# A fifth row buffer for the whole kernel in place of a fourth pair of split trunk weights, tile 2's keys found beside its scores, and a closer plan for dense-stage rows

## The chip, the cores and the metric

One core of one Trainium2 chip. The metric is device time in microseconds, taken over several runs; a profile of one execution gives where it goes. TensorE (PE) multiplies matrices, VectorE (DVE), ScalarE (ACT) and GpSimd (POOL) work on tiles in on-chip memory, SyncE (SP) issues most transfers, and 16 DMA engines carry them. Each engine takes its own instructions in order and waits for others through semaphores.

## What is computed

One inference step of a one-layer hybrid model on 1024 prompt positions and 128 sample positions (9 tiles of 128 tokens; tile 0 is the sample). A trunk of large projections, gating and retention comes first, then a product-key retrieval over 16384 single-neuron experts. Of the latter:

```python
q = (t @ w_query).reshape(T, P_HEADS, P_DKEY)
s1 = jnp.einsum('thd,nd->thn', q[..., :P_HALF], k1)
s2 = jnp.einsum('thd,nd->thn', q[..., P_HALF:], k2)
v1, i1 = lax.top_k(s1, P_TOPK)
v2, i2 = lax.top_k(s2, P_TOPK)
cand = (v1[..., :, None] + v2[..., None, :]).reshape(T, P_HEADS, P_TOPK * P_TOPK)
vals, flat = lax.top_k(cand, P_TOPK)
...
a = jax.nn.gelu(jnp.einsum('td,thkd->thk', t, eu[experts]))
return jnp.einsum('thk,thkd->td', w * a, ev[experts])
```

Each token picks 8 x 16 = 128 experts, and each expert has a row of 1024 numbers in `eu` and one in `ev`.

## The kernel before

**Trunk.** The tiles go through in three groups: tiles 0 and 1, tiles 2 to 5, tiles 6 to 8. A group streams 128 weight units of 512 KB each. `take` (from L126) loads units ahead, splits each into a high and a low part (`whi` copied by ScalarE, `wlo` subtracted by VectorE, both in `split`, L200 and L204) and hands out the pair; three products on TensorE then stand for one of full precision. A unit of 512 columns is 24 products. Pairs are split up to unit n+2 when unit n is handed out, and `NPART` (L107) is the number of pairs that there is room for, 4. In the first group the row buffers `gat` also serve as places for raw weights (two units in each), so `n_raw` grows with their number `GB`.

**Two ways of retrieval.** For tiles 0, 1, 2, 6 and 7 the 128 experts of each token are gathered: step j (L786, issued by GpSimd) brings for each of 128 tokens one row of 2048 numbers, 1 MB in all, into a buffer `gat`; VectorE forms the dot product with the token (`dot`, L739), ScalarE the weight (`weigh`, L744 and L745), VectorE adds the weighted second half to `acc` (`add`, L749), and the buffer is free. That is 5 x 128 = 640 rows. Tiles 3, 4, 5 and 8 go through a dense stage at the end instead: for each of 128 blocks of 128 experts, 24 products (L1008) give the scores, these are multiplied by the retrieval weights, split, and 24 further products (L980) add to the outputs. A block's loads are 1 MB and an eighth of a 2 MB tile of weights.

**What sets the order.** The rows and the search for their experts are side work. Two lanes, `gather_all` and `prepare`, each carry a clock of planned microseconds; `advance` adds the trunk's or the dense stage's planned cost, and `run_side` lets a lane go on until its clock has caught up. A row counts `PACE` = 5.0 planned us; a dense block counts twice 5.12. That fixes the order in which the program is written. The scheduler of the framework then places instructions on the engines by priority and as buffers come free; dense work has a priority 200 instructions ahead, so rows fill what it leaves. A row's buffer is the resource that it has to wait for.

**Row buffers.** `GB` = 4 buffers `gat`, and `AHEAD` = 2: the dot product of a row follows two steps after its gather. From dense block 2 to dense block 124 in program order, `spare` gives a fifth buffer `gats` in the dense stage's own memory, taken by every fifth row of a tile, and `AHEAD` is 3.

**Keys.** `top_keys` finds the best 16 of 128 scores for both halves of a head with ten operations of VectorE and a cast. For the tiles in `EARLY` (0, 1 and 8) this is done in `scores` right where the query stage produces the scores; for the others the scores are stored (`ssp`), loaded back by `topk_units` and searched there, in the lane `prepare`. Its results `v12` and `i12` have two buffers.

Of the kernel before, what the change touches and what calls it, by code (L numbers as in the profile page):

```python
# [8 lines left out]
F32 = mybir.dt.float32  # L9
# [8 lines left out]
P = 128  # L18
D = 1024
# [3 lines left out]
PH, NKEYS, TOPK = 8, 128, 16  # L23
# [19 lines left out]

GATHER, DENSE = [0, 1, 2, 6, 7], [3, 4, 5, 8]

EARLY = [0, 1, 8]
TD = len(DENSE) * P
EC = 4
LT = 16
# [5 lines left out]
def step_kernel(ctx: ExitStack, tc: tile.TileContext, x, state, wall, wst, bs, rows, vec, cst, smp, cosd, sind, euv,  # L55
# [5 lines left out]
    peer = ctx.enter_context(tc.tile_pool(name="peer", bufs=1))  # L61
# [42 lines left out]
            order += [U_IN + 2 * (32 + cb), U_IN + 2 * (32 + cb) + 1, U_PA + 2 * cb, U_PA + 2 * cb + 1]  # L104
        order += [U_OUT + i for i in range(8)] + [U_Q + i for i in range(16)]
    per = len(order) // len(GROUPS)
    NRAW, NPART, NBK = 3, 4, 2  # L107
    GB = 4
    MIX = 3
    wst_ = {"take": 0, "load": 0, "split": 0}  # L110
    raws, parts = {}, {}
    n_raw = lambda n: 2 * GB + MIX if n < per - 2 else NRAW
    pair = None

    def load(n):
        nonlocal pair
        if n < per - 2 and n % 3 < 2:

            if n % 3 == 0:
                pair = peer.tile([P, 2, 4, 256], F32, name="gat", bufs=GB)  # L120
            t = pair[:, n % 3]
# [37 lines left out]
    def mm_us(n):  # L159
        return n / 2400.0  # L160
# [36 lines left out]
    def split(parts, src, scale=None):  # L197

        if scale is None:
            nc.scalar.copy(parts[0], src)  # L200
        else:
            nc.scalar.activation(parts[0], src, AF.Copy, scale=scale)
        if scale is None:
            nc.vector.tensor_tensor(parts[1], src, parts[0].bitcast(F32), op=OP.subtract)  # L204
        else:
            nc.vector.scalar_tensor_tensor(parts[1], src, scale, parts[0].bitcast(F32), op0=OP.mult, op1=OP.subtract)
# [377 lines left out]
    def query(gi, pl, tl, nt, T, tT, rs, unit):  # L584
        def scores(h, qh):
            for i, t in enumerate(tl):
# [5 lines left out]
                st = st.rearrange("p a b -> p (a b)")  # L592
                if t in EARLY:
                    top_keys(t, h, st)
# [20 lines left out]
            pass  # L615


    AHEAD = [2]
    PACE = [5.0]
    BOOST = [100]  # L620
    AB = 2
# [17 lines left out]
    def top_keys(t, h, src):  # L639

        if t not in early:
            early[t] = (peer.tile([P, 2, PH, TOPK], F32, name="v12", bufs=2),
                        peer.tile([P, 2, PH, TOPK], BF16, name="i12", bufs=2))
        v12, i12 = early[t]
        tmp = peer.tile([P, P], F32, name="ktmp")
        iu = peer.tile([P, 2, TOPK], U32, name="iu")
        for c in range(2):
            top16(src[:, c * P:(c + 1) * P], tmp, v12[:, c, h], iu[:, c])
        nc.vector.tensor_copy(i12[:, :, h], iu)
        keyed[t] = h + 1  # L650
# [84 lines left out]
    queue = []  # L735

    def dot(t, j, b):
        d = T_[t]
        nc.vector.tensor_tensor_reduce(out=b[:, :D], in0=b[:, :D], in1=d["x"], op0=OP.mult, op1=OP.add,  # L739
                                       scale=1.0, scalar=0.0, accum_out=d["s"][:, j:j + 1])  # L740

    def weigh(t, j, b):
        d = T_[t]
        nc.scalar.activation(d["s"][:, j:j + 1], d["s"][:, j:j + 1], AF.Gelu_apprx_tanh)  # L744
        nc.scalar.activation(d["s"][:, j:j + 1], d["s"][:, j:j + 1], AF.Copy, scale=d["w"][:, j:j + 1])  # L745

    def add(t, j, b):
        d = T_[t]
        nc.vector.scalar_tensor_tensor(d["acc"], b[:, D:], d["s"][:, j:j + 1], d["acc"], op0=OP.mult, op1=OP.add)  # L749
        if j == HK - 1:  # L750
            out_norm(d["acc"], peer.tile([P, 2 * D], F32, name="gat", bufs=GB), t)
            del T_[t]
# [3 lines left out]
    def gathered():  # L756

        last = list(dotted)
        dotted.clear()
        for cur in last:  # L760
            weigh(*cur)
        while len(queue) > AHEAD[0]:
            cur = queue.pop()
            if cur:
                dot(*cur)
                dotted.append(cur)
        for cur in last:
            add(*cur)

    spare = []  # L770

    def row_buffer(j):

        if spare and j % (GB + 1) == GB:
            return spare[0].tile([P, 2 * D], F32, name="gats", bufs=1)
        return peer.tile([P, 2 * D], F32, name="gat", bufs=GB)

    def gather(t):
        d = T_[t]
        d["x"] = peer.tile([P, D], F32, name="tx")  # L780
        nc.sync.dma_start(d["x"], tsp[t])
        d["acc"] = peer.tile([P, D], F32, name="acc", bufs=2)
        nc.sync.dma_start(d["acc"], xsp[t])
        for j in range(HK):
            b = row_buffer(j)
            nc.gpsimd.indirect_dma_start(out=b, out_offset=None, in_=euv,  # L786
                                         in_offset=bass.IndirectOffsetOnAxis(ap=d["idx"][:, j:j + 1], axis=0))
            queue.insert(0, (t, j, b))
            gathered()
            yield PACE[0]  # L790
# [55 lines left out]
    def out_norm(acc, tmp, t):  # L846

        nc.sync.dma_start(tmp[:, D:], row_bcast(rows, 2))
        final_norm(acc, tmp[:, :D], tmp[:, D:], t)
# [61 lines left out]
    def advance(c):  # L911
        nonlocal tm
        tm += c
        flush()
        run_side(tm)
# [31 lines left out]
    dp = dense_sb.enter_context(tc.tile_pool(name="dp", bufs=1))  # L947
# [9 lines left out]
    def fetch(name, e):  # L957
        if e < NKEYS:
            raw[name, e] = wp.tile([P, D], F32, name="wraw", bufs=RWB)
            nc.sync.dma_start(raw[name, e], eud[e].rearrange("p k e -> p (k e)") if name == "eu" else evd[e])  # L960

    def split_u(e):
        if e < NKEYS:
            eu[e] = [wp.tile([P, D], F32R, name=n, bufs=EUB) for n in ("whi", "wlo")]
            split(eu[e], raw.pop(("eu", e)))

    def split_v(e):
        r = raw.pop(("ev", e))
        ev[e] = []
        for j in range(2):  # L970
            h = [dp.tile([P, 512], F32R, name=f"ev{j}{m}", bufs=(2, NBK + 1)[j]) for m in range(2)]
            split(h, r[:, 512 * j:512 * j + 512])
            ev[e].append(h)
# [8 lines left out]
    def block(o, es):  # L982
        ps = dps.tile([P, 512], F32, name="blk")
        for e in es:
            value(ps, o, e, e == es[0], e == es[-1])
        if es[0] == 0:
            nc.vector.tensor_copy(oacc[o], ps)
        else:
            nc.vector.tensor_tensor(oacc[o], oacc[o], ps, op=OP.add)

    us = 24 * mm_us(TD)
    todo = []
    hp = ExitStack()
    hp.enter_context(tc.high_priority(DP))
# [4 lines left out]
    for e in range(NKEYS + 1):  # L999
        if e < NKEYS:  # L1000
            if e % BE == 0:
                pt = dp.tile([P, TD // LT, BE, LT], F32, name="pt", bufs=2)
                nc.sync.dma_start(pt.rearrange("p c e t -> p c (e t)"), pdr[e // BE])
            ps = dps.tile([P, TD], F32, name="S")
            for k in range(KD):
                w, a = [p[:, k * P:(k + 1) * P] for p in eu[e]], [p[:, k] for p in tT]
                for i, (x, y) in enumerate(((w[0], a[0]), (w[1], a[0]), (w[0], a[1]))):
                    mm(ps, x, y, start=k == 0 and i == 0, stop=k == KD - 1 and i == 2)  # L1008
            del eu[e]
            fetch("ev", e + 1)  # L1010
            fetch("eu", e + 2)
            a = dp.tile([P, TD], F32, name="a", bufs=2)
            nc.scalar.activation(a, ps, AF.Gelu_apprx_tanh)  # L1013
            r16 = lambda z: z.rearrange("p (c t) -> p c t", t=LT)
            nc.vector.tensor_tensor(r16(a), r16(a), pt[:, :, e % BE], op=OP.mult)
            G[e] = [dp.tile([P, TD], F32R, name=f"g{m}", bufs=NBK + 1) for m in range(2)]
            split(G[e], a)
            split_v(e)
            split_u(e + 2)
            if e == 2:  # L1020
                spare.append(dp)
                AHEAD[0] = 3
            if e == NKEYS - 4:
                spare.clear()
                AHEAD[0] = 2
            hp.close()
            advance(us)
            hp.enter_context(tc.high_priority(DP))
        if todo:
            block(*todo.pop())  # L1030
        if e:
            for o in held:
                value(res[o], o, e - 1, e == 1, e == NKEYS)
            if e % NBK == 0 or e == NKEYS:
                es = list(range((e - 1) // NBK * NBK, e))
                if len(blocked) > 0:
                    block(blocked[0], es)
                if len(blocked) > 1:
                    todo.append((blocked[1], es))
            hp.close()  # L1040
            advance(us)
            hp.enter_context(tc.high_priority(DP))
# [98 lines left out]
```

## Time and profile before

| | us |
|---|---|
| median of 3 runs | 4063.04 (4037.91 to 4064.33) |
| the profiled execution, its own time | 4061.48 |
| its span, first to last instruction | 4059.4 |
| TensorE busy | 3655.6 (90% of the span) |
| VectorE busy | 3459.1 (85%) |
| ScalarE busy | 1846.8 (45%) |
| GpSimd busy | 980.0 (24%) |

The groups of tiles take 15 to 543 us, 543 to 1520 us and 1520 to 2350 us; up to 2490 us tile 8 is prepared for the dense stage, which then lasts to 3990 us, and the rest belongs to the last rows. Busy time is time in which an instruction of the engine runs; products are pipelined, so that their durations overlap (0.39 us each, one every 0.23 us). An engine's wait is told with the instruction that waited and the one, or the transfer, that ended it.

### The profile page before, as it was taken

The page shows a single profiled execution, that of the slowest core. Times are in us where ns is not written, and L with a number is a line of the kernel's source. Part 1 is how long each engine was busy: PE and PEld are TensorE (multiplying, and loading weights), DVE is VectorE, ACT ScalarE, POOL GpSimd, SP SyncE. Part 2 cuts the span into 40 slices and gives each one's busy share as a digit, 9 for nine tenths or more (in the row PEclk, how much of TensorE's full clock was granted, in tenths as well). Part 3 has the DMA queues.
Part 4 walks back from the last instruction along what each step waited for, and adds up shares of the span by engine and source line. Part 5 has one row for each costly group of instructions (what it writes and reads, how often), then busy time and mean ns, then how long its engine had stood idle before and what let it go on. Part 6 is the DMA issues. An engine that isn't in the chain of part 4 may idle for free.

```text
span 4059.4 us, 55000 instructions
## 1 busy us (share of the span) xinstructions
PE 3655.6 (90%) x19724; PEld 3088.0 (76%) x19724; DVE 3459.1 (85%) x6439; ACT 1846.8 (45%) x3879; POOL 980.0 (24%) x740
## 2 busy tenths in 40 slices
PE   8999999989989878989989858999999999999993
PEld 6779987867877767878989846777777777777772
DVE  5556699888888779989888888999999999888887
ACT  4435544444343443665657655434333334333332
POOL 0110002333333220021221202343213333322232
PEclk9999999999989989999989978999999999999996
DMA  8665637898989975585777836999969999998987
GB/s 286 210 215 192 225 122 288 317 339 316 334 308 332 352 272 176 158 295 199 260 259 254 305 129 235 382 379 385 356 245 373 388 373 381 353 341 330 337 326 282
DMA packets 247602, 1178.14 MB, mean 290 GB/s; under 512 B 28448, under 2 KB 47648, under 8 KB 163360
## 3 DMA queue, kind: packets, MB, share of 16 engines
q0 software_dynamic: 105984, 721.47, 48.1%
q1 hardware_dynamic: 141344, 453.16, 30.9%
q8 instruction: 155, 2.54, 0.2%
q14 instruction: 119, 0.97, 0.1%
HBM read 1096.92 MB, written 77.59 MB: 289 GB/s over the span
## 4 chain that ended last, share of the span: by engine, by line
issue 31%; PE 24%; DVE 17%; POOL 13%; DMA 12%; ACT 3%; POOLq 0%; SPq 0%; ACTq 0%; DVEq 0%
POOL gat L786 12%; PE gps L176 6%; PE S L1008 5%; PE gps L192 4%; PE res L980 4%; DMA gat<-in_euv_dram,idx 3%; DMA pdr<-st 3%; DVE wlo L204 3%; DVE acc L749 2%; DMA wraw<-in_evd_dram 2%; DVE gat L739 1%; PE sps L397 1%; DMA s<-ssp 1%; PE sps L395 1%; PE blk L980 1%
## 5 line engine op out<-in xcount | busy, mean ns | idle before, releaser
L786 POOL DMA_INDIRECT gat<-in_euv_dram,idx x591 | 834.8, 1413 | 2409.6 <-DVE acc L749 1629.5
L739 DVE CUSTOM_DVE_ANT_0 gat<-gat,tx 128x1024 f32<-128x1024 f32 x591 | 719.7, 1218 | 173.7 <-DMA gat<-in_euv_dram,idx 158.4
L980 PE MATMUL res<-ev,g 128*128 128x512 f32 x2304 | 812.3, 395 | 24.1 <-ACT g L200 21.1
L1008 PE MATMUL S<-h,whi 128*128 128x512 f32 x2048 | 766.5, 401 | 30.1 <-ACT a L1013 26.0
L749 DVE SCALAR_TENSOR_TENSOR acc<-gat,sdot,acc 128x1024 f32<-128x1024 f32 x591 | 755.3, 1278 | 22.0 <-ACT sdot L745 21.2
L192 PE MATMUL gps<-whi,h 128*128 128x256 f32 x3456 | 657.5, 289 | 16.7 <-DVE rot L302 10.0
L744 ACT ACTIVATE sdot<-sdot 128x1 f32<-128x1 f32 x640 | 128.4, 202 | 1050.2 <-DVE sdot L739 1049.0
L192 PEld LDWEIGHTS gps<-whi,h 128*128 128x128 f32 x3456 | 554.3, 195 | 39.4 <-issue 30.7
L204 DVE TENSOR_TENSOR wlo<-wraw,whi 128x1024 fp32r<-128x1024 f32 x428 | 521.0, 1218 | 64.7 <-ACT whi L200 63.3
L200 ACT CAST whi<-wraw 128x1024 fp32r<-128x1024 f32 x428 | 446.2, 1044 | 210.5 <-PE gps L176 89.7
L980 PEld LDWEIGHTS res<-ev,g 128*128 128x128 f32 x2304 | 434.1, 190 | 135.4 <-ACT g L200 35.6
L176 PE MATMUL gps<-h,whi 128*128 128x256 f32 (+2 forms) x1920 | 498.6, 342 | 4.0 <-ACT pb L328 3.8
L192 PE MATMUL gps<-wlo,h 128*128 128x256 f32 x1728 | 497.9, 288 | 4.3 <-DVE wlo L204 4.3
L1008 PEld LDWEIGHTS S<-h,whi 128*128 128x128 f32 x2048 | 390.2, 191 | 142.1 <-ACT a L1013 58.8
L176 PE MATMUL gps<-y,whi 128*128 128x256 f32 (+2 forms) x1536 | 407.7, 347 | 27.0 <-ACT y L200 6.5
L1008 PE MATMUL S<-h,wlo 128*128 128x512 f32 x1024 | 404.0, 395 | 0.0
L176 PEld LDWEIGHTS gps<-h,whi 128*128 128x128 f32 x1920 | 343.6, 192 | 32.0 <-ACT pb L328 4.3
L192 PEld LDWEIGHTS gps<-wlo,h 128*128 128x128 f32 x1728 | 336.9, 195 | 16.2 <-issue 10.7
L176 PE MATMUL gps<-h,wlo 128*128 128x256 f32 (+2 forms) x960 | 327.1, 341 | 0.5 <-DVE wlo L204 0.5
L176 PEld LDWEIGHTS gps<-y,whi 128*128 128x128 f32 x1536 | 277.7, 194 | 54.6 <-ACT y L200 7.1
L200 ACT CAST ev<-wraw 128x512 fp32r<-128x512 f32 x256 | 158.0, 621 | 236.2 <-PE res L980 103.3
L176 PE MATMUL gps<-y,wlo 128*128 128x256 f32 (+2 forms) x768 | 264.5, 345 | 0.0
(220 smaller groups left out, 5465.6 us busy)
## 6 DMA issues: line engine op xcount, KB each, us to landing
wraw<-in_wall_dram SPq DMA_DIRECT2D x300, 512.0 KB, 5.0
wraw<-in_eud_dram SPq DMA_DIRECT2D x128, 512.0 KB, 7.3
wraw<-in_evd_dram SPq DMA_DIRECT2D x128, 512.0 KB, 7.1
gat<-in_wall_dram SPq DMA_DIRECT2D x84, 512.0 KB, 4.6
pdr<-st POOLq DMA_DIRECT2D x32, 1024.0 KB, 8.4
pt<-pdr SPq DMA_DIRECT2D x16, 2048.0 KB, 12.5
Sb<-in_state_dram SPq DMA_DIRECT2D x64, 256.0 KB, 3.7
out_dram<-Sb POOLq DMA_DIRECT2D x64, 256.0 KB, 3.2
```

The costliest lines, as they stand in the source:

```text
L176: mm(ps[:, c, :T], x, y, start=kh == 0 and k == 0 and j == 0, stop=kh == nk - 1 and k == 3 and j == len(pr) - 1)
L192: mm(ps[:, i], y, x, start=kh == 0 and k == 0 and j == 0 and i % 2 == 0, stop=kh == 1 and k == 3 and j == len(pr) - 1 and last)
L200: nc.scalar.copy(parts[0], src)
L204: nc.vector.tensor_tensor(parts[1], src, parts[0].bitcast(F32), op=OP.subtract)
L395: mm(pu, x, y, start=j == 0, stop=j == 2)
L397: mm(po[r:r + 2 * LS], qm[:, c, b], Sb, start=False, stop=b % 2 == 1 and c == 1)
L739: nc.vector.tensor_tensor_reduce(out=b[:, :D], in0=b[:, :D], in1=d["x"], op0=OP.mult, op1=OP.add, scale=1.0, scalar=0.0, accum_out=d["s"][ ...
L744: nc.scalar.activation(d["s"][:, j:j + 1], d["s"][:, j:j + 1], AF.Gelu_apprx_tanh)
L749: nc.vector.scalar_tensor_tensor(d["acc"], b[:, D:], d["s"][:, j:j + 1], d["acc"], op0=OP.mult, op1=OP.add)
L786: nc.gpsimd.indirect_dma_start(out=b, out_offset=None, in_=euv, in_offset=bass.IndirectOffsetOnAxis(ap=d["idx"][:, j:j + 1], axis=0))
L980: mm(ps, x, y, start=start and i == 0, stop=stop and i == 2)
L1008: mm(ps, x, y, start=k == 0 and i == 0, stop=k == KD - 1 and i == 2)
```

## The change

`EARLY` takes in tile 2, so that its keys are found in the query stage of the second group, without the store and load of its scores. `NPART` falls from 4 to 3 and `GB` rises from 4 to 5: a pair of split weights and a row buffer take 8 KB per partition each. `AHEAD` is 3 from the first row to the last, and the buffer `gats` in the dense stage with its `spare` is gone; all rows take the five buffers in turn. `PACE` is 4.6 from the dense stage on. With `GB` the raw weights ahead in the first group rise from 11 to 13.

```diff
-EARLY = [0, 1, 8]
+EARLY = [0, 1, 2, 8]
...
-    NRAW, NPART, NBK = 3, 4, 2
-    GB = 4
+    NRAW, NPART, NBK = 3, 3, 2
+    GB = 5
...
-    AHEAD = [2]
+    AHEAD = 3
...
-        while len(queue) > AHEAD[0]:
+        while len(queue) > AHEAD:
...
-    spare = []
-
-    def row_buffer(j):
-
-        if spare and j % (GB + 1) == GB:
-            return spare[0].tile([P, 2 * D], F32, name="gats", bufs=1)
-        return peer.tile([P, 2 * D], F32, name="gat", bufs=GB)
...
-            b = row_buffer(j)
+            b = peer.tile([P, 2 * D], F32, name="gat", bufs=GB)
...
     us = 24 * mm_us(TD)
+    PACE[0] = 4.6
...
             split_u(e + 2)
-            if e == 2:
-                spare.append(dp)
-                AHEAD[0] = 3
-            if e == NKEYS - 4:
-                spare.clear()
-                AHEAD[0] = 2
             hp.close()
```

## Rows read from the trace of the kernel before

**Rows 1.** Busy time by stage. Columns: stretch, its length, busy us (and instructions) of PE, PE's weight loads, DVE, ACT and POOL, granted clock, DMA share, GB/s.

```profile
543.00:1520.00 977.00, 875.38 (x4798) 738.31 (x4798) 841.08 (x1368) 394.99 (x851) 279.73 (x202) 0.94 0.83 306
1520.00:2350.00 830.00, 743.16 (x4797) 698.94 (x4797) 728.42 (x1816) 504.06 (x1037) 148.99 (x107) 0.95 0.69 237
...
3543.00:3990.00 447.00, 412.74 (x1708) 320.27 (x1706) 388.14 (x517) 160.70 (x379) 135.90 (x102) 0.98 0.90 332
3990.00:4060.00 70.00, 3.25 (x8) 1.82 (x6) 50.18 (x66) 18.53 (x48) 18.24 (x12) 0.53 0.71 266
```

**Rows 2.** The products of L1008 (24 to a block) in three stretches of the dense stage. Columns: stretch, length, busy us and number of the products and of their weight loads, granted clock, DMA share, GB/s.

```profile
2500.00:2900.00 400.00, 284.68 (x847) 155.87 (x845) 1.00 0.98 376
...
3600.00:3900.00 300.00, 191.22 (x558) 106.07 (x558) 0.97 0.90 333
...
3543.00:3990.00 447.00, 287.15 (x840) 158.15 (x840) 0.98 0.90 332
```

**Rows 3.** The gathers of L786 in two of these stretches. Columns: stretch, length, POOL's busy us and the number of gathers, then as before.

```profile
2500.00:2900.00 400.00, 151.57 (x101) 1.00 0.98 376
...
3600.00:3900.00 300.00, 88.41 (x68) 0.97 0.90 333
```

**Rows 4.** All engines in the same two stretches, columns as in rows 1.

```profile
2500.00:2900.00 400.00, 393.27 (x1704) 315.39 (x1703) 388.26 (x516) 157.76 (x373) 151.57 (x101) 1.00 0.98 376
...
3600.00:3900.00 300.00, 273.58 (x1115) 210.87 (x1113) 255.43 (x341) 107.53 (x252) 88.41 (x68) 0.97 0.90 333
```

**Rows 5.** The gathers into the fifth buffer over the whole span (shortest, median and longest ns, then the first and last start), and the time from issue to landing of all gathers.

```profile
L786 POOL DMA_INDIRECT gats<-in_euv_dram,idx x49: 939/1677/1728, 2483.1 to 3543.0; - x49
...
DMA to landing us min/median/max: 5.5/8.4/15.4
```

**Rows 6.** Who waited for whom from 3600 to 3900 us: us in total, times, longest.

```profile
DVE gat L739 <- DMA gat<-in_euv_dram,idx: 37.2, 19, 3.5
```

**Rows 7.** The gathers of L786 by stage, columns as in rows 3.

```profile
543.00:1520.00 977.00, 279.73 (x202) 0.94 0.83 306
...
3543.00:3990.00 447.00, 135.90 (x102) 0.98 0.90 332
3990.00:4060.00 70.00, 18.24 (x12) 0.53 0.71 266
```

**Rows 8.** The end: the products of L980 over the span (the last start is the last figure of the first row's times), two of the last gathers, and an addition between them. Columns of the last three: start, duration, engine, instruction, idle time before it and what ended that.

```profile
L980 PE MATMUL res<-ev,g x2304: 387/389/792, 2492.9 to 3989.3; 128*128 128x512 f32 x192
...
4032.51 1.68 POOL L786 DMA_INDIRECT gat<-in_euv_dram,idx  x1 [1.35 <-DVE acc L749]
4035.54 1.68 POOL L786 DMA_INDIRECT gat<-in_euv_dram,idx  x1 [1.35 <-DVE acc L749]
...
4033.98 1.28 DVE L749 SCALAR_TENSOR_TENSOR acc<-gat,sdot,acc 128x1024 f32<-128x1024 f32 x1 [0.60 <-ACT sdot L745]
```

**Rows 9.** VectorE's groups of instructions from 2500 to 2900 us: number, busy us, mean ns of one, idle time before them.

```profile
L749 DVE SCALAR_TENSOR_TENSOR acc<-gat,sdot,acc 128x1024 f32<-128x1024 f32 x81 | 103.6, 1278 | 0.0
L739 DVE CUSTOM_DVE_ANT_0 gat<-gat,tx 128x1024 f32<-128x1024 f32 x78 | 94.9, 1216 | 0.0
L204 DVE TENSOR_TENSOR ev<-wraw,ev 128x512 fp32r<-128x512 f32 x69 | 46.9, 686 | 9.4 <-ACT ev L200 9.2
L204 DVE TENSOR_TENSOR wlo<-wraw,whi 128x1024 fp32r<-128x1024 f32 x35 | 42.6, 1218 | 0.5 <-ACT whi L200 0.4
```

**Rows 10.** Waits from 543 to 1520 us, of VectorE and of PE: us in total, times, longest.

```profile
DVE gat L739 <- DMA gat<-in_euv_dram,idx: 86.1, 65, 3.8
...
PE sps L402 <- DVE sc L359: 18.3, 2, 10.1
PE sps L503 <- DVE va L483: 16.5, 1, 16.5
...
PE gps L192 <- DVE wlo L204: 2.4, 1, 2.4
```

**Rows 11.** The wait of VectorE on rows from 1500 to 2320 us.

```profile
DVE gat L739 <- DMA gat<-in_euv_dram,idx: 17.3, 7, 5.5
```

**Rows 12.** Two units of split weights of the second group in order of time (ScalarE's copy, then VectorE's subtraction of the same unit), two products of one unit 15 products apart, and ScalarE's wait for PE from 1500 to 2320 us. Columns of the first six: start, duration, engine, instruction.

```profile
1179.17 1.04 ACT L200 CAST whi<-wraw 128x1024 fp32r<-128x1024 f32 x1
...
1180.10 0.39 PE L176 MATMUL gps<-h,wlo 128*128 128x512 f32 x1
...
1182.81 1.22 DVE L204 TENSOR_TENSOR wlo<-wraw,whi 128x1024 fp32r<-128x1024 f32 x1
...
1183.49 0.39 PE L176 MATMUL gps<-h,wlo 128*128 128x512 f32 x1
...
1185.17 1.04 ACT L200 CAST whi<-wraw 128x1024 fp32r<-128x1024 f32 x1
...
1192.56 1.22 DVE L204 TENSOR_TENSOR wlo<-wraw,whi 128x1024 fp32r<-128x1024 f32 x1
...
ACT whi L200 <- PE gps L176: 34.3, 17, 6.3
```

**Rows 13.** Operations of the search for keys over the span: number, shortest, median and longest ns, first and last start.

```profile
L631 DVE MAX8 v<-s x96: 267/279/427, 1420.8 to 2962.4; 128x8 f32<-128x128 f32 x96
...
L635 DVE FIND_INDEX8 iu<-v,ktmp x144: 275/285/623, 500.9 to 2966.5; 128x8 uint32<-128x128 f32 x144
...
L649 DVE CAST i<-iu x72: 153/174/491, 502.4 to 2966.9; 128x32 bf16<-128x32 uint32 x72
```

## The prediction

> **What bounds the kernel now.** I read the busy time of each engine by stage first, then stretches inside the dense stage, then the waits in them, and last the end. One profiled execution has a span of 4059.4 us and a time of 4061.48 us, so 2.1 us lie around the span; the median of the runs shown is 4063.04 us, 1.6 us above. The sums below are made against 4061.5 us.
>
> By stage [rows 1], the first wide group (543 to 1520 us) has PE busy 875 of 977 us and DVE 841; the second (1520 to 2350) PE 743 and DVE 728 of 830. In the dense stage the reader should compare two stretches with the same code [rows 2 to 4]. In 2500 to 2900, 847 products of L1008 at 24 to a block are 35.3 blocks, so 11.33 us a block, and 101 rows are gathered (25.3 per 100 us); PE is busy 98%, DVE 97%. In 3600 to 3900, 558 products are 23.3 blocks, 12.90 us each, with 68 rows (22.7 per 100 us); PE 91%, DVE 85%.
>
> What differs between them is the fifth row buffer. Its last gather starts at 3543.0 [rows 5]. The rows run ahead of the planner: the 250 or so planned between blocks 2 and 124 (122 x 10.24 planned us / 5.0) are used up near block 93 (840 products, 35 blocks, are still to come [rows 2]), and everything later has four buffers and AHEAD 2. There a row is wanted two steps after its gather, 2 x 300/68 = 8.8 us, while the median landing is 8.4 us and the longest 15.4 us [rows 3, 5]. So VectorE, which works in order, waits: 37.2 us in 300 [rows 6], and PE loses about the same (300 - 23.3 x 11.33 = 36 us). With five it is wanted three steps later, 3 x 400/101 = 11.9 us. The end shows the same thinness: the dense products stop at 3989, 12 gathers start after 3990, and the last of them go 3.03 us apart, each addition waiting 0.60 us on ScalarE [rows 7, 8].
>
> **The change, part by part.** *Five buffers in the rest of the dense stage.* From 3543 there are 35 blocks left, which took 447 us [rows 2]. At 11.33 us they take 397: 50 us less. The rows then decide whether that holds: 102 + 12 = 114 are left [rows 7], and 397 us at 25.3 per 100 carries 100, so some 14 remain for the end, as now. Seen from VectorE: a row is 1.28 + 1.22 us, a block 1.22 + 5 x 0.69 us (the full-width split, two ev splits, product, split of G and the addition, all of the ev row's size) [rows 9]. Their plain sum for 2500 to 2900 is 101 x 2.50 + 35.3 x 4.67 = 417 us against 388 busy [rows 4], so ends overlap and the factor is 0.93: 2.33 us a row, 4.34 us a block. The rest is 114 x 2.33 + 35 x 4.34 = 417 us, and about 10 us for the dense outputs; at 97% busy that is 440 us, plus some 10 us for the last norm: end at 3994, 65 us earlier. From the rows' own pace it is 50 us and 14 rows x (3.03 - 2.33) = 10 us, so 60. I take 60; bounds 45 (the last rows keep 3.03 and a little of the blocks' pace is lost) and 65.
>
> *Five buffers in the trunk.* The same wait costs VectorE 86.1 us in the first wide group [rows 10] and 17.3 us in the second [rows 11], 103 together. All of it is the upper bound, nothing the lower: PE's own longest waits there are for VectorE's sc and va, 35 us [rows 10], and the split weights stand some units ahead, so a late VectorE does not always stop PE, which waited for wlo itself 2.4 us in all there [rows 10]. But whatever VectorE gains is not lost: if the trunk does not end sooner, more rows are done in it, and each is 2.33 us less in a dense stage where VectorE is 97% busy. I take half, 50 us.
>
> *Three pairs of split weights.* With four, the split of unit n+2 may start when unit n-2 is done; with three, when n-1 is done, so the pair has two units of PE time to be ready. A unit of the first wide group is 24 products of (1183.49 - 1180.10)/15 = 0.226 us [rows 12], 5.4 us, so two are 10.8; in the second, with 384 columns, estimated at 3/4 of that, 8.1. The work is 1.04 us on ScalarE and 1.22 on VectorE, but both queue: two units show 4.9 us (1179.17 to 1184.03) and 8.6 us (1185.17 to 1193.78) from the start of one to the end of the other [rows 12]. The slow one fits 10.8 and misses 8.1 by 0.5 us. Behind a waiting copy on ScalarE stand the evictions and the weighing of rows, which PE and the additions wait for; ScalarE already waits 34.3 us in 17 places for PE to free a pair in the second group [rows 12]. Lower bound nothing; upper bound 0.5 us on all 256 units of the two groups, 128 us. I take 20 us, near the lower end: a unit must be as slow as the second of these two to miss at all, part of what made it slow are the waits on rows that now go, and PE's wait of 2.4 us for wlo [rows 10] tells how rarely pairs are short today. In the first group of units nothing else competes, and I take nothing there.
>
> *Tile 2's keys.* 8 heads x (2 x 5 operations x 0.28 + 0.17) = 24 us of VectorE [rows 13] move from the second wide group, where VectorE is 88% busy, to the query stage at the end of the first, where it has room; eight stores and eight loads of 128 KB go from SP's queue. The scores' buffers are then held until the keys are found, not until a store lands. Between 24 us gained and 24 lost; I take 10 gained.
>
> *The pace.* 4.6 for 5.0 puts 1311 x (1/4.6 - 1/5.0) = 23 rows more ahead of the stage's end in program order (1311 is 128 blocks of 10.24 planned us). But rows already run some 30 blocks ahead of 5.0, so free buffers set their order and not the plan, and I take nothing. Bounds: 23 x (3.03 - 2.33) = 16 us gained, or 23 x 2.33 = 54 us lost if each stood in front of a block's own work.
>
> Sum: 60 + 50 - 20 + 10 = 100 us, so 4061.5 - 100 = 3961, say 3960 us.
>
> A rule that speaks against the dense term: what binds there may be the DMA engines and not the buffers, since their share is 0.98 in 2500 to 2900 at 376 GB/s [rows 4]. The 447 us at 332 GB/s and 70 at 266 [rows 1] are 167 MB; at 376 GB/s that is 444 us, end at 3987 plus the last norm, 62 us earlier: the same term again. The Trainium skill (DMA: Bandwidth & Descriptors, section Specifications) puts HBM's share for one core at about 358 GB/s; this trace shows 376, so it disagrees. By the page's figure an estimate of 466 us would end at 4019, 40 us earlier.
>
> **The rivals.** *Only the dense term comes* (VectorE's trunk waits are hidden by the weights ahead, and the DMA engines stay the bound): 60 us, 4000 us. For it: PE waits seldom name a row. Chance 0.17.
>
> *The trunk eats the gain:* three pairs cost 0.25 us a unit more than the waits give, 256 x 0.25 = 64 us against 60: about 4060; with part of it 4040. Chance 0.15.
>
> *Slower:* the same ring, worse, in one place: ScalarE's copy of unit n+2 waiting for unit n-1 in front of evictions. It decides from (60 + 41) / 256 = 0.39 us a unit; at the upper bound of 0.5 us with no trunk gain, 4061.5 - 60 + 128 = 4130. Against it: two units minus the plain 2.26 us leave 8.5 and 5.8 us for queueing. Chance 0.07.
>
> *The row is in time already,* so the change does nothing for it: if a row landed within its two steps wherever it is wanted, four buffers would do, and 20 us of the ring stay: 4070. The 37.2 and 86.1 us of waits speak against it; chance 0.03. By the Trainium skill (the same page, section "Anatomy of one DMA, SWDGE (gpsimd) path": 2.0 us and the bytes at 436 GB/s) a row of 1 MB would land in an estimated 4.4 us; the trace, with 8.4 us, disagrees.
>
> *More than forecast:* all of the 103 us used and no loss by the ring: 60 + 103 + 10 = 173, but PE's 128 blocks at 11.33 us from 2490, 3940, and 25 us of end set a floor of 3965 unless the trunk ends sooner; with it 50 us sooner, 3915. Chance 0.11.
>
> **How the numbers follow.** The forecast has 0.47: 3960 us, its own range 3925 to 4000. Range 3900 to 4050: it leaves out the slower case, the case in time already, and some of the edges. About 1% (41 us) is what a measurement of this kernel can tell from no change. Faster: 0.47 + 0.17 + 0.11 and 0.02 of the trunk rival = 0.77. Same: 0.13 + 0.03 = 0.16. Slower 0.07.
>
> **What would show it.** Right: after the dense stage is two thirds through, blocks still 11.3 us apart with 25 rows per 100 us and no wait of VectorE on a row; in the first wide group that wait well under 86 us, and either its end before 1520 or more than 202 rows in it; the rows at the end under 3 us apart. The ring right: PE's waits on wlo or whi stay under 20 us. Wrong: PE busy in the trunk falls, ScalarE's wait for PE at whi grows several times over, or the dense stage begins after 2520.

## The result, and the profile after

The changed kernel takes 3954.24 us (median of 4 runs, 3949.41 to 3961.46) against 4063.68 us for the kernel before: a ratio of 0.9744, 95% interval 0.9706 to 0.9781. That is 2.6% or 104 us by the ratio. The forecast was 3960 us.

Busy time by stage of the profiled execution, whose span is 3947.5 us; the columns are those of [rows 1]. The stages are cut at the first products of the second and the third group of tiles (here called the first wide group, tiles 2 to 5, and the second, tiles 6 to 8), the last product of the trunk, the first score product of the dense stage, a point 1053 us into it, and its last product.

```profile
546.00:1458.00 912.00, 857.80 (x4793) 728.72 (x4793) 840.71 (x1369) 394.14 (x852) 306.37 (x205) 0.96 0.87 329
1458.00:2303.00 845.00, 751.43 (x4813) 705.40 (x4813) 751.84 (x1837) 511.26 (x1059) 169.04 (x119) 0.95 0.72 247
2303.00:2455.00 152.00, 62.71 (x318) 56.32 (x316) 129.27 (x464) 91.46 (x213) 26.91 (x19) 0.64 0.54 183
2455.00:3508.00 1053.00, 1017.48 (x4341) 814.26 (x4342) 996.22 (x1550) 415.59 (x942) 350.35 (x238) 0.98 0.93 357
3508.00:3935.00 427.00, 419.28 (x1805) 334.93 (x1803) 387.14 (x519) 165.61 (x382) 134.22 (x92) 1.00 0.88 338
3935.00:3948.00 13.00, 0.00 (x0) 0.00 (x0) 8.15 (x12) 4.63 (x10) 0.00 (x0) 0.66 0.50 202
```

The kernel before, from its second wide group on, cut at the same events. The cuts of [rows 1] lie a little elsewhere: the first score product starts at 2475.6 us and not at 2490 (second block), and products run to 4000 us and not to 3990.

```profile
1520.00:2353.00 833.00, 746.16 (x4814) 701.94 (x4814) 728.42 (x1816) 504.06 (x1037) 148.99 (x107) 0.95 0.69 236
2353.00:2476.00 123.00, 60.13 (x317) 54.36 (x316) 100.21 (x427) 84.45 (x182) 8.13 (x8) 0.69 0.38 117
...
3529.00:4000.00 471.00, 429.99 (x1775) 333.42 (x1773) 407.89 (x546) 171.16 (x401) 141.64 (x106) 0.97 0.90 334
4000.00:4060.00 60.00, 0.00 (x0) 0.00 (x0) 43.86 (x56) 14.05 (x40) 17.30 (x11) 0.50 0.68 254
```

```profile
L1008 PE MATMUL S<-h,whi x2048: 387/389/797, 2475.6 to 3982.0; 128*128 128x512 f32 x187
```

The first wide group takes 912 us where it took 977 [rows 1], and VectorE is busy for the same 841 us in both: it had waited. Of the 65 us, 48 are time in which PE stood idle (54 us for 102). The other 17 are PE's own busy time (858 us for 875, the same products), at a mean granted clock of 0.96 for 0.94 of full speed: the lower of its two levels, 1.2 GHz, was granted for less of the time. The second wide group takes 845 us for 833 and the stretch before the dense stage 152 for 123, so that the dense stage begins 21 us earlier. The end after the last product takes 13 us for 60. In the last stage of the dense work PE is busy 98% for 91%. The first group (tiles 0 and 1) ends at 546 us for 543, so its two more places for raw weights bring nothing.

The gathers in the first three of these stages (POOL's busy us and their number, as in [rows 7]; one that lies across a cut is counted on both sides):

```profile
546.00:1458.00 912.00, 306.37 (x205) 0.96 0.87 329
1458.00:2303.00 845.00, 139.84 (x95) 0.95 0.72 247
2303.00:2455.00 152.00, 18.58 (x12) 0.64 0.54 183
```

Counted from the end, 640 - 237 - 92 = 311 gathers start ahead of the dense stage: 237 start from 2455 to 3508 us and 92 later. In the kernel before the numbers are

```profile
2476.00:3529.00 1053.00, 347.93 (x239) 0.99 0.93 359
3529.00:4000.00 471.00, 141.64 (x106) 0.97 0.90 334
```

and 11 after 4000 us, so 640 - 239 - 106 - 11 = 284. So 27 rows more are started by then. The first wide group did about as many as before (205 for 202) in 65 us less.

From 3600 to 3900 us, the products of L1001 (L1008 before), the gathers of L778 (L786 before), and VectorE's wait on rows, beside [rows 2, 3, 6]:

```profile
3600.00:3900.00 300.00, 212.38 (x639) 117.71 (x639) 1.00 0.93 358
```

```profile
3600.00:3900.00 300.00, 100.94 (x69) 1.00 0.93 358
...
L778 POOL DMA_INDIRECT gat<-in_euv_dram,idx x640: 932/1676/3482, 600.8 to 3869.7; - x160
```

```profile
DVE gat L739 <- DMA gat<-in_euv_dram,idx: 4.6, 4, 2.8
```

639 / 24 = 26.6 blocks are 11.27 us apart, where the kernel before had 12.90 [rows 2]. The wait on rows is 4.6 us for 37.2 [rows 6]. The last gather starts at 3869.7, some 65 us before the last product, so the 69 rows are not a rate: none is left at the end.

Waits from 546 to 1458 us, of VectorE on rows and of PE on low parts and on VectorE's `va` and `sc`, beside [rows 10]:

```profile
DVE gat L739 <- DMA gat<-in_euv_dram,idx: 30.9, 30, 4.8
```

```profile
PE sps L503 <- DVE va L483: 7.0, 1, 7.0
...
PE gps L176 <- DVE wlo L204: 4.7, 2, 4.1
...
PE sps L402 <- DVE sc L359: 4.0, 2, 2.7
PE gps L192 <- DVE wlo L204: 3.0, 2, 2.4
```

### The profile page after: what moved, and what is told of

It reads as the page before. It is cut to its first block, busy times and chain, and to the rows that moved or that the text cites. A ratio compares the mean times of both kernels' runs of the same rounds, so it can differ in the third digit from the quotient of the medians.

```text
span 3947.5 us, 54950 instructions
## 1 busy us (share of the span) xinstructions
PE 3636.9 (92%) x19724; PEld 3085.6 (78%) x19724; DVE 3450.0 (87%) x6439; ACT 1847.1 (47%) x3879; POOL 1022.0 (26%) x740
## 4 chain that ended last, share of the span: by engine, by line
issue 34%; PE 19%; POOL 16%; DVE 16%; DMA 11%; ACT 3%; POOLq 0%; SPq 0%; DVEq 0%; ACTq 0%
POOL gat L778 16%; PE gps L176 6%; DMA pdr<-st 4%; PE gps L192 4%; DMA gat<-in_euv_dram,idx 3%; DVE acc L749 2%; PE S L1001 2%; DVE wlo L204 2%; DVE gat L739 2%; PE res L972 2%; PE sps L397 1%; PE sps L395 1%; DMA s<-ssp 1%; ACT st L806 1%; DVE ktmp L633 1%
## 5 line engine op out<-in xcount | busy, mean ns | idle before, releaser
L778 POOL DMA_INDIRECT gat<-in_euv_dram,idx x640 | 948.2, 1482 | 2378.8 <-DVE acc L749 1639.5
L739 DVE CUSTOM_DVE_ANT_0 gat<-gat,tx 128x1024 f32<-128x1024 f32 x640 | 782.6, 1223 | 68.7 <-DMA gat<-in_euv_dram,idx 52.7
L749 DVE SCALAR_TENSOR_TENSOR acc<-gat,sdot,acc 128x1024 f32<-128x1024 f32 x640 | 821.4, 1283 | 1.3 <-ACT sdot L745 0.9
L972 PE MATMUL res<-ev,g 128*128 128x512 f32 x2304 | 802.4, 393 | 8.8 <-ACT g L200 8.6
L1001 PE MATMUL S<-h,whi 128*128 128x512 f32 x2048 | 758.8, 398 | 10.0 <-ACT a L1006 5.9
L972 PEld LDWEIGHTS res<-ev,g 128*128 128x128 f32 x2304 | 433.2, 189 | 111.5 <-ACT g L200 17.9
L1001 PEld LDWEIGHTS S<-h,whi 128*128 128x128 f32 x2048 | 388.2, 190 | 118.6 <-ACT a L1006 33.3
L1001 PE MATMUL S<-h,wlo 128*128 128x512 f32 x1024 | 402.0, 393 | 0.0
```

Of the source, the lines that this page charges most:

```text
L972: mm(ps, x, y, start=start and i == 0, stop=stop and i == 2)
```

## The experiments

Two theories stood against each other. Mine: free row buffers set the rate of the side work, so that the fifth one pays both late in the dense stage and in the trunk, the ring of three pairs gives a little back, and the keys and the pace matter little. The rivals: the closer plan or the early keys bring the rows forward, and that alone cures the end. All ratios are to the kernel before.

### e1: the pace left at 5.0

```diff
-    PACE[0] = 4.6
```

> The changed kernel with the dense-stage pace left at 5.0. Theory (free buffers set the rows' order, not the plan): no difference, 3954 us within 0.5%, all rows still gathered before the dense products stop. Rival (the closer plan is what brings the rows in before the end): 23 rows more are left for the end at 2.4 to 3.0 us each, so 3954 + 55 to 70 = about 4015 us, with a tail of gathers after the last product.

3953.69 us, 0.9741 (0.9721 to 0.976). The changed kernel's own time, and the gathers start in the same stages in the same numbers: 205, 94 and 12 ahead of the dense stage, 237 in its first 1053 us, 92 later. The pace does nothing that can be told.

### e2: tile 2's keys in the side lane

```diff
-EARLY = [0, 1, 2, 8]
+EARLY = [0, 1, 8]
```

> The changed kernel with tile 2's keys searched in the side lane again (EARLY = 0, 1, 8). Theory: 24 us of VectorE work go back from the end of the second group of tiles into the third, worth about 10 us: 3964 us. Rival (the early keys bring the gain before the dense stage): the second group's end goes back by most of its 62 us and the rows done at the start of the dense stage fall from 311 towards 284, so about 4000 to 4030 us.

3957.05 us, 0.9747 (0.973 to 0.9764). The rival fails, and my 10 us are not seen either: 1 us by the ratios, 3 by the medians, inside both intervals. The intervals reach 0.4% (15 us) to either side for the changed kernel and 0.2% (7 us) here, so 10 us are not ruled out.

### e3: three pairs alone

```diff
-    NRAW, NPART, NBK = 3, 4, 2
+    NRAW, NPART, NBK = 3, 3, 2
```

> The kernel before with three pairs of split weights and nothing else. Theory (three pairs cost a little, mostly in the third group of tiles): 4063 + 10 to 40 us = about 4085 us; PE's waits for wlo in the third group (2 us before, 21 us in the changed kernel) come up here too, the first group stays the same. Rival (the ring costs nothing and the longer third group of the changed kernel comes from more rows in it): 4063 us within 0.5%, third group as before.

4077.43 us against 4058.96, 1.0048 (1.0033 to 1.0062): 19 us lost. The size is as expected, the place is not. PE's waits from 544 to 1535 us, its first wide group:

```profile
PE gps L176 <- DVE wlo L204: 15.9, 8, 5.4
PE gps L192 <- DVE wlo L204: 13.7, 5, 7.4
```

29.6 us of waits for low parts where [rows 10] has 2.4. The two wide groups by stage:

```profile
544.00:1535.00 991.00, 878.13 (x4803) 739.56 (x4801) 846.61 (x1363) 398.93 (x856) 285.60 (x204) 0.94 0.82 304
1535.00:2370.00 835.00, 748.63 (x4817) 703.77 (x4816) 726.18 (x1811) 500.11 (x1031) 140.48 (x105) 0.95 0.68 234
```

991 us for 977 and 835 for 833: the loss lies in the first wide group, which I had thought safe with 10.8 us for a pair.

### e4: the fifth buffer to the end, in the dense stage alone

`dp` is closed with the dense stage; `dq` is memory that is open before it and to the end.

```diff
             if e == 2:
-                spare.append(dp)
+                spare.append(dq)
                 AHEAD[0] = 3
-            if e == NKEYS - 4:
-                spare.clear()
-                AHEAD[0] = 2
```

> The kernel before with its fifth row buffer, and AHEAD 3, held from dense block 2 to the last row (the buffer comes from memory that lives to the end), nothing else changed. Theory (the late dense stage and the end lose by four buffers): trunk as before, blocks 11.3 us apart after 3543 instead of 12.8, rows at the end under 3 us apart, 60 us gained: about 4003 us (3998 to 4018). Rival (the gain at the end of the changed kernel comes only from the 27 rows done earlier): the dense stage keeps its 12.8 us a block late, about 4050 us.

4009.0 us, 0.9874 (0.9855 to 0.9893): 51 us gained. From 3600 to 3900 us, the products of L1008 (first row) and the gathers (second), then VectorE's waits on rows:

```profile
3600.00:3900.00 300.00, 214.62 (x638) 117.54 (x638) 1.00 0.98 383
...
3600.00:3900.00 300.00, 108.10 (x77) 1.00 0.98 383
```

```profile
DVE gats L739 <- DMA gats<-in_euv_dram,idx: 1.3, 1, 1.3
DVE gat L739 <- DMA gat<-in_euv_dram,idx: 0.5, 1, 0.5
```

26.6 blocks 11.29 us apart and 77 rows, 25.7 per 100 us: with nothing changed but the buffer and the AHEAD 3 that goes with it, the pace of [rows 2, 3] for five is there to the end, and the wait of 37.2 us is down to 1.8.

It is not quite the dense stage alone. The fifth buffer is in use from 2355.8 us on: nine rows start between the trunk's last product and the first score product, where none did before, and that stretch takes 139 us for 123. From the first score product to the end of the profile it is 1511 us for 1584. So more is gained there than the 51 us, and part is lost ahead of it.

### e5 and e9: four buffers for the last rows of the changed kernel

In both, pace 5.0, and from dense block 124 in program order:

```diff
+            if e == NKEYS - 4:
+                kept = peer.tile([P, 2 * D], F32, name="gat", bufs=GB)
+                nc.vector.memset(kept[:, :1], 0.0)
+                AHEAD[0] = 2
```

e5 writes `kept` once more with a constant after all lanes are done; e9 instead after the last dense products:

```diff
+    for o in blocked:
+        nc.vector.tensor_copy(kept[:, :1], oacc[o][:, :1])
```

> The changed kernel with pace 5.0, and from dense block 124 in program order one of the five row buffers set aside and AHEAD 2, so that the last 110 or so rows have four buffers as in the kernel before; the trunk keeps five. Theory (late dense stage and trunk gain apart from each other): trunk as in the changed kernel with about 311 rows at the start of the dense stage, late blocks slower again and a longer end, so 3954 + 40 to 55 = about 4000 us; the trunk's part alone is then about 60 us. Rival (rows brought forward by the trunk already cure the late stage): 3954 to 3970 us.

> As e5, but the row buffer that is set aside at dense block 124 in program order is now written once more from the last dense outputs, so that it stays taken to the end of the dense stage (in e5 it came free again at 3430 us and the late rows had five buffers after all). Theory (rate of rows and pace of blocks in the late dense stage follow the number of buffers): late blocks go to 12 us or more apart, gathers 4.4 us instead of 3.9 us apart, some rows are left after the last product: 3954 + 30 to 55 = about 3995 us. Rival (with 311 rows done at its start the late stage no longer needs the fifth buffer): 3954 to 3965 us.

e5: 3954.56 us, 0.9762 (0.9735 to 0.9789). It tests less than was meant. The two writes to the buffer set aside (start and duration in ns, first and last start in us):

```profile
L1014 DVE MEMSET gat<- x1: 59/59/59, 3424.5 to 3424.5; 128x1 f32 x1
...
L1052 DVE MEMSET gat<- x1: 59/59/59, 3430.1 to 3430.1; 128x1 f32 x1
```

They lie 6 us apart, so the fifth buffer was gone only that long, and what is left of the edit is AHEAD 2 for the last rows (and the pace of e1), which changes nothing.

e9: 4015.95 us, 0.9897 (0.9867 to 0.9928). From 3600 to 3900 us, products of L1000, gathers, and the wait on rows:

```profile
3600.00:3900.00 300.00, 191.80 (x560) 105.72 (x560) 0.97 0.89 331
...
3600.00:3900.00 300.00, 90.57 (x67) 0.97 0.89 331
```

```profile
DVE gat L739 <- DMA gat<-in_euv_dram,idx: 32.8, 18, 4.8
```

These are the numbers of the kernel before, nearly to the digit: 12.86 us a block, 22.3 rows per 100 us, 32.8 us of waits [rows 2, 3, 6]. So the late fifth buffer is worth 0.9897 - 0.9744 = 1.5%, 62 us (by the two intervals give or take 20), in the changed kernel, and the rows that the trunk brings forward don't replace it. This time the buffer stays set aside:

```profile
L1014 DVE MEMSET gat<- x1: 59/59/59, 3436.9 to 3436.9; 128x1 f32 x1
```

The next writes to it come at 3997.9 us. It is gone 106 us earlier than the last gather into `gats` in the kernel before (3543.0, [rows 5]), so 62 us is somewhat more than the term of the forecast covers.

What the rest of the change brings is then 1 - 0.9897 = 1.0%, 42 us; with the 19 us that e3 shows for the ring, five buffers in the trunk and the keys bring some 61 us, if the parts add. In the profile of e9 311 rows start ahead of the dense stage, none is left after the last product, and the end takes 13 us, all as in the changed kernel: with four late buffers too, the 27 rows of the trunk shorten the end.

### e6: five buffers, AHEAD 2

```diff
-    AHEAD = 3
+    AHEAD = 2
```

> The changed kernel with AHEAD 2, still five buffers. Theory (a free buffer lets GpSimd issue the gather early; the step at which the dot product is written matters little): 3954 to 3965 us, VectorE's waits on rows stay under 80 us. Rival (the number of steps between gather and dot product is what covers the landing, as the reasoning 2 x 4.4 us against 8.4 us has it): the waits come back to 150 us and the time to about 4010 us.

3951.34 us, 0.9747 (0.9719 to 0.9776): no difference. VectorE's dot products over the span (busy us, mean ns, idle before them and what ended it):

```profile
L739 DVE CUSTOM_DVE_ANT_0 gat<-gat,tx 128x1024 f32<-128x1024 f32 x640 | 779.7, 1219 | 66.6 <-DMA gat<-in_euv_dram,idx 46.1 <-DMA tx<-tsp 20.1
```

46.1 us of waits on rows over the whole kernel (52.7 in the changed one, 158.4 for `gat` in the kernel before). From 3550 to 3800 us a dot product starts 12.0 us on average after the start of its gather, and 12.6 us in the changed kernel. The number of steps between gather and dot product in the program is not what covers the landing; the buffer is.

### e7 and e10: one more high part, or one more low part

```diff
-            hi, lo = (wp.tile([P, 4, 256], F32R, name=n, bufs=NPART) for n in ("whi", "wlo"))
+            hi, lo = (wp.tile([P, 4, 256], F32R, name=n, bufs=b) for n, b in (("whi", 4), ("wlo", 3)))
```

e10 has 3 and 4.

> The changed kernel with four high parts and three low parts of split weights (4 KB more). Theory (the ring's cost comes from ScalarE's copy standing in its queue until PE frees a pair, with evictions and row weights behind it): ScalarE's waits for PE at whi in the first wide group fall from 102 us towards 50, and 5 to 15 us are gained: 3940 to 3949 us. Rival (VectorE's subtraction then waits in its place, with rows behind it): VectorE's wait for PE at wlo appears, 3954 us or more.

> The changed kernel with three high and four low parts of split weights, the mirror of e7. Theory (the ring's cost is ScalarE's copy waiting in its queue for PE): nothing gained, 3950 to 3958 us, ScalarE's waits for PE at whi in the first wide group stay near 100 us. Rival (any more room in the ring gives the 30 us): 3920 to 3935 us.

e7: 3923.98 us, 0.9678 (0.9661 to 0.9696), clear of the changed kernel's interval: 0.66% or 27 us better, more than the 5 to 15 expected. e10: 3950.56 us, 0.9741 (0.9712 to 0.9769), no difference. ScalarE's waits at the copies of high parts in the first wide group, first the changed kernel, then e7:

```profile
ACT whi L200 <- PE gps L176: 66.3, 20, 11.6
ACT whi L200 <- PE gps L192: 35.9, 18, 4.5
```

```profile
ACT whi L200 <- DMA wraw<-in_wall_dram: 62.0, 17, 11.8
ACT whi L200 <- PE gps L176: 40.4, 18, 4.4
ACT whi L200 <- PE gps L192: 14.0, 7, 4.7
```

The waits for PE fall from 102 to 54 us as expected, but 62 us of waits for raw weights (8.8 in the changed kernel) stand in their place. By stage e7 gains elsewhere:

```profile
545.00:1462.00 917.00, 854.55 (x4798) 726.60 (x4798) 843.21 (x1375) 398.38 (x855) 304.19 (x205) 0.97 0.87 328
1462.00:2289.00 827.00, 748.70 (x4811) 705.61 (x4810) 749.27 (x1833) 514.82 (x1058) 171.10 (x117) 0.95 0.72 250
```

The first wide group is 5 us longer than in the changed kernel; the second takes 827 us for 845, and the rest of the 24.6 us of this profile's span (3922.9 for 3947.5) comes after it. From 1458 to 2299 us VectorE's subtraction waits less for the copy, first the changed kernel, then e7:

```profile
DVE wlo L204 <- ACT whi L200: 38.9, 17, 5.8
```

```profile
DVE wlo L204 <- ACT whi L200: 9.1, 8, 2.0
```

(e7 from 1462 to 2289 us.) So the gain of 27 us is shown, but not that it comes the way of the theory: where the waits of the expectation fell, no time was gained, and in the second wide group the chain from PE over the copy to VectorE fits, but is not shown.

### e8: four pairs, paid by a raw weight buffer

```diff
-    NRAW, NPART, NBK = 3, 3, 2
+    NRAW, NPART, NBK = 2, 4, 2
```

> The changed kernel with four pairs of split weights again, paid by two instead of three raw weight buffers (a 512 KB unit lands in 4 to 5 us, a unit takes 5.4 us in the first wide group and about 4.1 in the other). Theory (the fourth pair is worth the 19 us that taking it away cost alone, and raw weights need two places): about 3940 us. Rival (raw weights come late and ScalarE waits for them): ScalarE's wait for wraw grows from under 30 us to over 60, 3960 us or more.

3945.1 us, 0.9745 (0.9722 to 0.9767). By the ratio no difference. The rival's sign is there without its time: ScalarE's waits for raw weights in the first wide group (548 to 1468 us) and the second (1468 to 2304 us), 8.8 and 6.5 us in the changed kernel, are 132.2 and 125.2 us. What the fourth pair gives, the third raw buffer seems to have been worth as well. That was not taken apart.

### e11: e7 with more priority for tile 8

```diff
-    BOOST = [100]
+    BOOST = [1000]
```

> e7's kernel with the priority of the side work on tile 8 before the dense stage raised from 100 to 1000 instructions. In the changed kernel that stretch takes 152 us with 12 rows in it, 123 us with none before. Theory (each row there delays the stretch by its 2.3 us of VectorE): rows leave the stretch, it shortens towards 125 us, 10 to 25 us are gained: about 3905 us. Rival (it is ScalarE's expansion that sets its length): 3924 us, stretch still about 150 us.

3917.19 us, 0.9656 (0.9629 to 0.9684): the fastest median of all, but not to be told from e7. The second wide group, and the stretch before the dense stage:

```profile
1458.00:2281.00 823.00, 748.34 (x4814) 703.24 (x4813) 749.71 (x1839) 514.80 (x1058) 171.57 (x117) 0.96 0.71 252
2281.00:2427.00 146.00, 64.59 (x317) 58.45 (x316) 123.29 (x461) 90.55 (x207) 22.50 (x17) 0.63 0.52 176
```

146 us for 149 in e7 and 152 in the changed kernel, not 125: priority does not clear the stretch of its rows (9 start in it, 10 in e7), so this run does not test what a row costs there. All runs side by side do. From the trunk's last product to the first score product it is 122 or 123 us where no row starts in between (the kernel before, e3, e12), 139 to 146 with 9 (e4, e2, e11), 149 with 10 (e7), and 150 to 155 with 12 (the changed kernel and the other six). That is (152 - 123) / 12 = 2.4 us a row, close to the 2.33 us of VectorE that the prediction counts for one. No run changes the rows of this stretch alone.

### e12: the kernel before with four high and three low parts

The edit of e7 on the kernel before.

> The kernel before with four high and three low parts of split weights; beside e3, which has three of both and came to 1.0048 of the kernel before. Theory (three pairs cost through ScalarE's copy, which stands in its queue until PE frees a pair): the high parts' fourth place takes back most of the 19 us, 4055 to 4068 us and a ratio of 0.999 to 1.001. Rival (the missing low part costs it, through VectorE's subtraction, for which PE waited 30 us in e3's first wide group against 2 us before): ratio 1.003 to 1.006, PE's waits for wlo stay near 30 us there.

4080.53 us against 4059.32, 1.0056 (1.0042 to 1.007): the rival. PE's waits on low parts from 545 to 1525 us:

```profile
PE gps L176 <- DVE wlo L204: 15.6, 6, 5.6
...
PE gps L192 <- DVE wlo L204: 7.5, 3, 6.8
```

23.1 us, near the 29.6 of e3. In the kernel before, the missing low part alone costs what the whole pair costs (21 and 19 us), and a fourth high part takes nothing back. The waits are a sign and not the price: in this profile the first wide group takes 979 us for 977 and the second 840 for 833. In the changed kernel it is the high part that pays and the low part that does not. My theory on ScalarE's queue fits the second alone. Why the two kernels differ stays open.

## Why the prediction was right, point by point

**Late dense stage, 60 us.** Shown: 51 us alone (e4), 62 us as the last part (e9, a longer stretch). Of the working, the pace of 11.3 us a block held (11.27 and 11.29). That 14 rows would stay for the end did not hold: none stays in the changed kernel. Either part is nearly enough for that: e4, without the trunk's rows, has one row left, and e9, with them but with four late buffers, has none. The end itself was read too long: the products that stop at 3989 us are those into `res`, those into `blk` go on to 4000, so it took 60 us and not 70; now it takes 13.

**Five buffers in the trunk, 50 us.** Some 61 us with the keys, by difference and not by a run of its own: the other parts of the change were put back or tried one by one (e1, e2, e3, e6), and no run has the fifth buffer in the trunk alone. The forecast had 50 and 10 us for the two; the 50 were half of an upper bound, so that this part of the sum came out is in some measure luck. The gain came in two forms that the forecast had named together: 65 us in the first wide group, and 27 rows more ahead of the dense stage. PE's longest waits there were not only those named: it waited 18.5 us for ScalarE's `st` (L591), 6.8 after the change, and the 34.8 us for `sc` and `va` [rows 10] fell to 11.0.

Part is given back: 12 us in the second wide group and 29 us in the stretch before the dense stage, which now has 12 rows in it; e11 tells what the runs show of these. The 29 us were not foreseen. The first 1053 us of the dense stage go nearly as before, (3072 - 886)/24 = 91.1 blocks for 2206/24 = 91.9. The rows are the score products after them in the changed kernel, and those in them before:

```profile
3508.00:3935.00 427.00, 296.36 (x886) 163.71 (x884) 1.00 0.88 338
```

```profile
2476.00:3529.00 1053.00, 738.08 (x2206) 412.54 (x2205) 0.99 0.93 359
```

**Three pairs, 20 us lost.** 19 us alone (e3). The size was right, the place only in part: I put the loss into the second wide group, by a unit of 8.6 us against 8.1, and called the first safe with 10.8. In the kernel before it lies in the first (e3). In the changed kernel the first is 65 us shorter all the same, the second takes 845 us for 833, and 827 with a fourth high part (e7). PE's waits for split weights, which were to stay under 20 us, are 8.8 us in the first wide group and 23.0 in the second. The reason, copies on ScalarE with evictions behind them, fails in the kernel before (e12) and in the first wide group of e7; it fits the second. So only the size is shown.

**Keys, 10 us.** Not to be told from nothing, nor from 10 (e2). **Pace, nothing.** Nothing that can be told (e1).

**The mechanism of the wait.** The prediction explained the 37.2 us by steps: a row wanted two steps after its gather, 8.8 us, against a landing of 8.4. That step failed. With AHEAD 2 and five buffers the waits stay away (e6), with AHEAD 2 and four in the end they come back (e9). GpSimd starts a gather as soon as an addition frees a buffer, in the changed kernel too:

```profile
3704.65 1.67 POOL L778 DMA_INDIRECT gat<-in_euv_dram,idx  x1 [4.86 <-DVE acc L749]
3706.99 1.14 POOL L778 DMA_INDIRECT gat<-in_euv_dram,idx  x1 [0.67 <-DVE acc L749]
```

The traces give the turn of a buffer, if the buffers are taken in order. Averages of the rows from 3600 to 3900 us:

| | four buffers (the kernel before; e9 within 0.1) | five (e4) |
|---|---|---|
| start of the gather to start of the dot product | 9.9 us | 12.2 us |
| from there to the end of the addition | 7.7 us | 7.1 us |
| from there to the gather that takes the buffer next | 0.3 us | 0.3 us |
| a whole turn | 17.9 us | 19.6 us |
| landing of the row after its issue | 8.0 us | 9.2 us |

So no buffer lies idle for long, and the rate is the number of buffers over the turn: 22.3 and 25.5 rows per 100 us. The turn is not fixed: a fifth buffer makes it 1.7 us longer, so the rate grows by about 15% and not by 25%. A landed row lies ready for 2 us on average with four buffers and for 3 us with five.

**The rivals.** "Only the dense term comes" is refuted by e4 beside the changed kernel (0.9874 against 0.9744). "The trunk eats the gain" and "slower" were priced on the ring, which costs 19 us. The row is not "in time already", by e9.

## What to carry to other kernels

When a gather's buffer is refilled the moment it is freed, its rate is buffers divided by the time of one turn, and one more buffer lengthens the turn. A stretch of the same kernel that already runs with one more buffer prices the change before it is made, and here that price, 60 us, held within 10 us. Memory for it came from a ring on which PE waited 2.4 us in 977; that cost 19 us. Take the parts of such a ring apart: in the changed kernel, giving back one half of one pair was worth 27 us more, the other half nothing. Rows that are brought forward are not free where they land: here they made the stretch before the dense stage 29 us longer. What an edit writes into program order (steps, pace) may not reach the engines at all when a scheduler places instructions by free buffers; one run with the number changed back tells.

## What the runs showed of the hardware that was not expected

In e4 the DMA engines carried 383 GB/s from 3600 to 3900 us, with a share of 0.98, and 77 rows and 26.6 blocks went through; the changed kernel did as many blocks at 358 GB/s. There the rows ran out at 3869.7 us. So a share near 1 went with more rows done and not with later blocks: 11.29 us apart at 0.98, 11.27 us at 0.93. The Trainium skill (DMA: Bandwidth & Descriptors, section Specifications) gives about 358 GB/s as the limit of HBM for one core, worked out as half of what two cores share. The 383 GB/s here, with the program on one core, lie above it.
